# DeltaNet preparation: inverses of two heads in one instruction, half of the decays' rows on ScalarE, transposes one part later, a new order of the parts

## The chip, the cores and the metric

The kernel runs on one core of a Trainium2 chip, in one launch. The metric is the time of the device in microseconds. Five compute engines work from queues of their own and wait for one another by semaphores: TensorE (PE in the profile, with its weight loads as PEld), VectorE (DVE), ScalarE (ACT), GpSimd (POOL) and SyncE (SP), which issues the transfers here. Within one engine, instructions run in the order in which they stand in its queue.

## The reference

One layer of an encoder on 1024 + 256 tokens (two sequences with the same parameters), model width 1024. The mixing half of the layer has two groups: a gated DeltaNet with 4 heads of 128, run forwards and backwards in time, and an attention with 4 query heads and 2 key heads. An output projection and an MLP follow. The change lies in what the DeltaNet needs before its scan:

```python
h = RMSNorm_pre(x); p = h @ w_in
qkv = silu(conv(p_qkv))                 # centred, 5 taps, per channel
q = l2norm(q) * DK ** -0.5;  k = l2norm(k)
diff  = g_cumsum[:, None] - g_cumsum[None, :]
decay = where(lower, exp(diff), 0)      # per chunk, head and direction
kk    = (beta * k) @ k.T * decay
tri   = I + where(strict, kk, 0)
u, w  = solve(tri, [beta * v, beta * k * exp(g)])   # unit lower triangular
a_qk  = (q @ k.T) * decay
# scan over the chunks:  v_new = u - w S;  o = q_d S + a_qk v_new;  S = ...
```

The kernel solves with an explicit inverse of `tri`, in tiles of 128 tokens: 10 tiles, 4 heads, 2 directions.

## The kernel before

The stages of the span are the norm of x with the projection for z and the gates (0 to 111 us), the **preparation** (111 to 536), attention and DeltaNet scan side by side (536 to 800), then the output projection and the MLP. Only the preparation is touched.

It consists of parts, each a generator that is written out step by step. The string `ORDER` (L39 to L43) lists the steps: each entry runs its part up to the next `yield`. Instructions of neighbouring steps lie interleaved in the engines' queues, so a row of the order counts, not the string alone. The parts, for a head h or a column block j:

- **K** (`gdn_qk`): twice a projection with convolution (`conv_proj`), for k and for q. `proj_T` (L350 to L370) casts the weights (`whi` on ScalarE, `wlo` on VectorE at L80), runs 3 x 8 matmuls for each of the token ranges 512, 512 and 256 (`pt`, L367 to L369), and copies to `cp`. After that VectorE adds three taps (L443), GpSimd one (L444), and the SiLU ends on VectorE (L446). TensorE transposes the result by tiles (`kt` L459, `qt` L473), ScalarE takes squares (`gj`, L376) and scaled copies (`kn`, L464) that are stored in `vis_d`.
- **V** (`gdn_v`): the same for v, with transposes `vt` (L502) and copies `vn` (L505).
- **E** (`gdn_e`): five steps of two tiles. `pe` collects a mask (L516) and the decays, whose right-hand sides `ER` (L518) are the mask `incl` times gates: direction 0 on GpSimd, direction 1 on VectorE, 512 columns each. ScalarE takes `E = exp(pe)` (L523). `pk` (L528) is k against k and q; VectorE makes `A` (L529, stored to `vis_d`, one buffer) and `C` (L531).
- **S** (`gdn_sub`): the inverse of all 32 x 32 diagonal blocks of one head. ScalarE copies them (`Cc`, L545), VectorE transposes half (`Ct`, L547), a round trip through `c_d` (L549 to L554) brings them to 80 partitions, one block each. After that there are 31 elimination steps, each a product (`prod`, L560) and an addition (`Rm`, L561) on VectorE and a clearing on GpSimd (L562).
- **L** (`gdn_lev`): a second round trip (`r_d` L569, `Rc` L573, `Rt` L576), and two levels that assemble 64 and then 128 from the blocks (`ph`, `py`, `px`, then `ph2`, `py2`: L589 to L625). The finished `C` is stored at L629 and L630.
- **a** (`att_proj`): a projection for attention. j = 0 to 3 are queries, 4 and 5 keys, 6 and 7 values. The second step transposes (`at`, L400), and for j < 6 turns by the rotary tables (L415 to L417) and, for keys, multiplies by `prk` (L423, L426). The result is stored to `arot_d`; the attention loads it as `ax`.

PSUM has eight banks: three for `pt`, two (`tr`) for `pe` and `pk`, and one each for the transposes of K and V (`tq`), for L (`iv`) and for the attention's transposes (`at`).

Of the kernel before, what the change touches and what calls it, by code (L numbers as in the profile page):

```python
# [20 lines left out]
NT = 10  # L21
# [15 lines left out]


ORDER = (  # L39
    "K0 K0 K0 K0 E0 E0 E0 E0 K1 E0 K1 S0 K1 K1 L0 E1 E1 V0 V0 E1 E1 L0 E1 K2 K2 K2 K2 E2 E2 E2 V1 E2 E2 "  # L40
    "V1 S1 K3 S2 K3 K3 L1 L1 V2 K3 L2 V2 V3 V3 E3 L2 a0 a0 E3 E3 a4 E3 E3 a4 S3 L3 a5 L3 a5 a6 a6 a1 a1 "
    "a2 a2 a3 a3 a7 a7"
)  # L43
# [18 lines left out]
def build(ctx, tc, I, O):  # L62
# [11 lines left out]
    def f32(ap):  # L74
        return ap.bitcast(F32)
# [418 lines left out]
    def gdn_v(h):  # L494
        vT = gp.tile([128, 1282], F32, tag="vT", name="vT", bufs=1)
        yield from conv_proj(8 + h, vT)
        irk = irks[h]
        for t0 in range(0, NT, 4):
            n = min(4, NT - t0)
            tp = tq_tile("vt")  # L500
            for j in range(n):
                T.transpose(tp[:, j * 128:(j + 1) * 128], vT[:, col(t0 + j)], ident)  # L502
            vn = gp.tile([128, 4, 128], F32, tag="kn", name="vn", bufs=3)
            for j in range(n):
                S.activation(vn[:, j], tp[:, j * 128:(j + 1) * 128], AF.Copy, scale=irk[:, t0 + j:t0 + j + 1])  # L505
            SP.dma_start(out=vis_d[h][:, t0:t0 + n, 5], in_=vn[:, :n])

    def gdn_e(h):
# [3 lines left out]
        for t0, n in ((0, 2), (2, 2), (4, 2), (6, 2), (8, 2)):  # L512
            E = gp.tile([128, 2, 2, 128], F32, tag="E", name="E", bufs=2)
            pe = tr_tile("pe").rearrange("p (d j c) -> p d j c", d=2, j=2)
            for d in range(2):
                T.matmul(pe[:, d], lhsT=identr, rhs=nmask[:, 1 - d:2 - d].to_broadcast([128, 2, 128]), start=True, stop=False)  # L516
                R = gp.tile([128, 2, 2, 128], F32R, tag="ER", name="ER", bufs=1)
                (G if d == 0 else V).tensor_tensor(  # L518
                    R, incl[:, d][:, None, None, :].to_broadcast([128, 2, 2, 128]),
                    f32(gr[:, :, t0:t0 + 2, 4 * d + h])[:, :, :, None].to_broadcast([128, 2, 2, 128]), ALU.mult)  # L520
                for i in range(2):
                    T.matmul(pe[:, d], lhsT=(r_gt, r_lt)[d], rhs=R[:, i], start=False, stop=(i == 1))
            S.activation(E, pe, AF.Exp)  # L523
            A = gp.tile([128, 2, 2, 128], F32, tag="A", name="A", bufs=1)
            for j in range(n):
                t = t0 + j
                pk = tr_tile("pk")
                T.matmul(pk[:, 0:256], lhsT=qk[:, 1, col(t)], rhs=qk[:, :, col(t)], start=True, stop=True)  # L528
# [9 lines left out]

    def gdn_sub(h):
        C = Cs[h]  # L540

        Cc = gp.tile([128, 2, NT, 32], F32, tag="Cc", name="Cc", bufs=1)
        for b in range(4):
            bs = slice(32 * b, 32 * b + 32)
            S.mul(Cc[bs], C[bs, :, :, bs].rearrange("p t d c -> p d t c"), -1.0)  # L545
        Ct = gp.tile([128, NT, 32], F32, tag="Ct", name="Ct", bufs=1)
        V.transpose(Ct.rearrange("p t c -> p (t c)"), Cc[:, 0].rearrange("p t c -> p (t c)"))  # L547
        c_d = dr.tile([128, 2, NT, 32], F32, tag="c_d", name="c_d", bufs=2)
        SP.dma_start(out=c_d[:, 0], in_=Ct)  # L549
        SP.dma_start(out=c_d[:, 1], in_=Cc[:, 1])  # L550

        Rm = gp.tile([80, 32, 32], F32, tag="Rm", name="Rm", bufs=2)
        for b in range(4):
            SP.dma_start(out=Rm[20 * b:20 * b + 20], in_=c_d[32 * b:32 * b + 32].rearrange("j d t i -> (d t) j i"))  # L554
        G.memset(Rm.rearrange("p a b -> p (a b)")[:, 0:1024:33], 1.0)
        for p in range(31, 0, -1):
            n = 32 - p
            prod = gp.tile([80, 256], F32, tag="prod", name="prod", bufs=2)
            pv = prod[:, :p * n].rearrange("q (j c) -> q j c", j=p)
            V.tensor_tensor(pv, Rm[:, p, 0:p][:, :, None].to_broadcast([80, p, n]), Rm[:, p:p + 1, p:].to_broadcast([80, p, n]), ALU.mult)  # L560
            V.tensor_tensor(Rm[:, 0:p, p:], Rm[:, 0:p, p:], pv, ALU.add)  # L561
# [933 lines left out]
```

## Time and profile before

| what | value |
|---|---|
| median of 3 runs | 1736.56 us (1734.45 to 1737.36) |
| the profiled execution's own time | 1741.06 us |
| its span, first to last instruction | 1739.3 us |
| mean granted TensorE clock | 0.981 |
| preparation, 111 to 536 us: PE, DVE, ACT, POOL busy | 380.5, 314.5, 226.3, 99.7 us |
| its granted clock and DMA share | 0.96, 0.45 |
| attention and scan, 536 to 800 us: PE busy | 246.1 us |
| from 800 us on: PE busy | 904.6 of 939 us |

"Busy" is the time in which an engine has at least one instruction running. TensorE's instructions overlap, so that their durations add up to more than the time between their starts. A row of a timeline gives start, length, engine, line, operation and tiles, a count where equal instructions follow each other, and in brackets how long the engine stood idle before it and what ended that.

### The profile page before, as it was taken

What the parts mean: (1) busy time and instruction counts of PE and PEld (TensorE: products, weight loads), DVE (VectorE), ACT (ScalarE), POOL (GpSimd) and SP (SyncE); (2) the same over time, 40 slices, a digit from 0 to 9 for tenths busy, and PEclk for the clock granted to TensorE, in tenths of its full rate; (3) what the DMA queues carried; (4) which work ended last, traced back from release to release, by engine and by line L of the source; (5) the groups of instructions that cost most, each with busy time, mean ns of one, the idle gap of its engine ahead of it and who ended that gap; (6) DMA issues with size and microseconds to landing.
All of it is one profiled execution on the core that took longest, in us unless ns stands there. A gap on an engine that the chain in (4) does not pass through costs nothing. (4 is left out here: it accounts for less than half of the span.)

```text
span 1739.3 us, 27944 instructions
## 1 busy us (share of the span) xinstructions
PE 1626.4 (94%) x9799; PEld 1387.8 (80%) x9799; DVE 1267.9 (73%) x2549; ACT 854.6 (49%) x1937; POOL 735.8 (42%) x658
## 2 busy tenths in 40 slices
PE   6999898898997999889988999999989999999997
PEld 5777776777775888668878999999888888888885
DVE  7546798996744778885759954545787978888777
ACT  5236566554345767674446644544465333333422
POOL 3212231321113334440102555554636777788763
PEclk9999999999998999999999999999999999999999
DMA  6113334445447866244333543444556544444234
GB/s 208 70 42 109 97 108 129 137 133 154 133 143 231 273 203 194 79 161 166 104 127 127 178 147 125 151 135 134 187 193 220 154 140 146 132 143 142 86 115 155
DMA packets 208779, 252.68 MB, mean 145 GB/s; under 512 B 35073, under 2 KB 163391, under 8 KB 208639
## 3 DMA queue, kind: packets, MB, share of 16 engines
q1 hardware_dynamic: 208495, 250.77, 45.9%
q8 instruction: 77, 1.26, 0.3%
q14 instruction: 63, 0.52, 0.1%
q0 software_dynamic: 144, 0.13, 0.0%
HBM read 159.75 MB, written 91.10 MB: 144 GB/s over the span
## 5 line engine op out<-in xcount | busy, mean ns | idle before, releaser
L1146 PE MATMUL pd<-mh,ulo 128*128 128x320 f32 x892 | 279.6, 314 | 12.9 <-DVE ulo L80 12.8
L1145 PE MATMUL pd<-mh,uhi 128*128 128x320 f32 x892 | 276.6, 311 | 5.5 <-ACT uhi L79 5.5
L1147 PE MATMUL pd<-ml,uhi 128*128 128x320 f32 x892 | 276.9, 311 | 0.0
L1289 DVE TENSOR_TENSOR acc<-acc,pd 128x512 f32<-128x512 f32 x330 | 206.7, 678 | 44.1 <-PE pd L1285 44.1
L1283 PE MATMUL pd<-dhi,fhi 128*128 128x512 f32 x490 | 192.2, 392 | 1.0 <-DVE acc L1291 1.0
L1284 PE MATMUL pd<-dl,fhi 128*128 128x512 f32 x490 | 192.3, 393 | 0.0
L1285 PE MATMUL pd<-dhi,flo 128*128 128x512 f32 x490 | 191.9, 392 | 0.0
L1146 PEld LDWEIGHTS pd<-mh,ulo 128*128 128x128 f32 x892 | 169.1, 190 | 17.8 <-DVE ulo L80 17.8
L367 PE MATMUL pt<-h_hi,whi 128*128 128x512 f32 (+1 forms) x480 | 178.5, 372 | 0.0
L369 PE MATMUL pt<-h_hi,wlo 128*128 128x512 f32 (+1 forms) x480 | 178.4, 372 | 0.0
L368 PE MATMUL pt<-h_lo,whi 128*128 128x512 f32 (+1 forms) x480 | 178.4, 372 | 0.0
L1145 PEld LDWEIGHTS pd<-mh,uhi 128*128 128x128 f32 x892 | 168.9, 190 | 7.0 <-ACT uhi L79 7.0
L1147 PEld LDWEIGHTS pd<-ml,uhi 128*128 128x128 f32 x892 | 169.0, 190 | 0.0
L1265 ACT CAST fhi<-fr 128x1280 fp32r<-128x1280 f32 x49 | 62.1, 1267 | 212.6 <-PE pd L1284 116.2
L80 POOL TENSOR_TENSOR dl<-dw,dhi 128x1024 fp32r<-128x1024 f32 x49 | 129.0, 2633 | 43.4 <-ACT dhi L79 42.8
L1190 POOL TENSOR_TENSOR s<-u,u 128x320 f32<-128x320 f32 x32 | 34.3, 1071 | 207.6 <-ACT u L1155 140.7
L727 POOL TENSOR_TENSOR P<-P,sm 128x512 f32<-128x512 f32 (+1 forms) x72 | 73.5, 1040 | 95.3 <-DVE sm L725 39.0
L1283 PEld LDWEIGHTS pd<-dhi,fhi 128*128 128x128 f32 x490 | 92.0, 188 | 22.4 <-DVE acc L1291 1.4
L1285 PEld LDWEIGHTS pd<-dhi,flo 128*128 128x128 f32 x490 | 92.0, 188 | 20.7
L1284 PEld LDWEIGHTS pd<-dl,fhi 128*128 128x128 f32 x490 | 92.0, 188 | 20.3
L80 DVE TENSOR_TENSOR ulo<-us,uhi 128x512 fp32r<-128x512 f32 x88 | 76.3, 869 | 43.4 <-ACT uhi L79 42.5
L367 PEld LDWEIGHTS pt<-h_hi,whi 128*128 128x128 f32 x480 | 92.7, 193 | 13.5
(358 smaller groups left out, 4091.0 us busy)
## 6 DMA issues: line engine op xcount, KB each, us to landing
fr<-r_d SPq DMA_DIRECT2D x49, 640.0 KB, 4.3
vis<-vis_d SPq DMA_DIRECT2D x64, 384.0 KB, 4.2
uraw<-in_w_up SPq DMA_DIRECT2D x22, 1024.0 KB, 5.4
r_d<-s SPq DMA_DIRECT2D x128, 160.0 KB, 1.8
r_d<-u SPq DMA_DIRECT2D x96, 160.0 KB, 2.1
dw<-in_w_down SPq DMA_DIRECT2D x28, 512.0 KB, 4.9
wraw<-in_w_in SPq DMA_DIRECT2D x48, 256.0 KB, 3.7
x<-in_x_prompt SPq DMA_DIRECT2D x16, 512.0 KB, 3.4
```

Source lines behind the costliest of these rows:

```text
L80: (V if leng is None else leng).tensor_tensor(lo, src, f32(hi), ALU.subtract)
L367: T.matmul(pm[:, :n], lhsT=whi, rhs=h_hi[:, k, t0:t0 + n], start=(k == 0), stop=False)
L368: T.matmul(pm[:, :n], lhsT=whi, rhs=h_lo[:, k, t0:t0 + n], start=False, stop=False)
L369: T.matmul(pm[:, :n], lhsT=wlo, rhs=h_hi[:, k, t0:t0 + n], start=False, stop=(k == KD - 1))
L727: G.tensor_tensor(x[:, :kw], x[:, :kw], sm[:, 0:1].to_broadcast([128, kw]), ALU.mult)
L1145: T.matmul(pm, lhsT=w[0][:, k], rhs=mh[b, i][:, k], start=(k == 0), stop=False)
L1146: T.matmul(pm, lhsT=w[1][:, k], rhs=mh[b, i][:, k], start=False, stop=False)
L1147: T.matmul(pm, lhsT=w[0][:, k], rhs=ml[b, i][:, k], start=False, stop=(k == 3))
L1283: T.matmul(pm, lhsT=r[0][:, k, tk], rhs=w[0][:, k], start=(k == 0), stop=False)
L1284: T.matmul(pm, lhsT=r[0][:, k, tk], rhs=w[1][:, k], start=False, stop=False)
L1285: T.matmul(pm, lhsT=r[1][:, k, tk], rhs=w[0][:, k], start=False, stop=(k == Q - 1))
L1289: V.tensor_tensor(half(t, d), half(t, d), pm, ALU.add)
```

## The change

Inverses (`gdn_sub`): a part now takes a pair of heads. `Rm` and `prod` get an axis of two, the 62 VectorE instructions become twice as long, and eight steps replace one; `Rm` has one buffer for the pair, `prod` one instead of two.

```diff
+        Rm = gp.tile([80, 2, 32, 32], F32, tag="Rm", name="Rm", bufs=1)
+        for i in range(2):
+            h = 2 * pair + i
...
+                SP.dma_start(out=Rm[20 * b:20 * b + 20, i], in_=c_d[32 * b:32 * b + 32].rearrange("j d t i -> (d t) j i"))
+            Rms[h] = Rm[:, i]
+        G.memset(Rm.rearrange("p h a b -> p h (a b)")[:, :, 0:1024:33], 1.0)
+        yield
         for p in range(31, 0, -1):
             n = 32 - p
-            prod = gp.tile([80, 256], F32, tag="prod", name="prod", bufs=2)
...
-            V.tensor_tensor(Rm[:, 0:p, p:], Rm[:, 0:p, p:], pv, ALU.add)
-            G.memset(Rm[:, p, 0:p], 0.0)
...
+            prod = gp.tile([80, 2, 256], F32, tag="prod", name="prod", bufs=1)
+            pv = prod[:, :, :p * n].rearrange("q h (j c) -> q h j c", j=p)
+            V.tensor_tensor(pv, Rm[:, :, p, 0:p][:, :, :, None].to_broadcast([80, 2, p, n]),
+                            Rm[:, :, p:p + 1, p:].to_broadcast([80, 2, p, n]), ALU.mult)
+            V.tensor_tensor(Rm[:, :, 0:p, p:], Rm[:, :, 0:p, p:], pv, ALU.add)
+            G.memset(Rm[:, :, p, 0:p], 0.0)
+            if p % 5 == 0:
+                yield
```

Decays (`gdn_e`): `ER` has two buffers, direction 0 is made by four ScalarE activations of 128 x 128, and `pk` moves from the ring `tr` to the ring of the transposes.

```diff
-                R = gp.tile([128, 2, 2, 128], F32R, tag="ER", name="ER", bufs=1)
-                (G if d == 0 else V).tensor_tensor(
...
+                R = gp.tile([128, 2, 2, 128], F32R, tag="ER", name="ER", bufs=2)
+                gd = f32(gr[:, :, t0:t0 + 2, 4 * d + h])
+                if d == 0:
+                    for i in range(2):
+                        for j in range(2):
+                            S.activation(R[:, i, j], incl[:, d], AF.Copy, scale=gd[:, i, j:j + 1])
...
-                pk = tr_tile("pk")
+                pk = tq_tile("pk")
```

PSUM: the three single banks become one ring of three.

```diff
-    tq_tile = b_tile("tq", 1)
-    iv_tile = b_tile("iv", 1)
-    at_tile = b_tile("at", 1)
+    tq_tile = iv_tile = at_tile = b_tile("fx", 3)
```

Transposes: K writes the projection for q before it finishes the convolution of k, and has a step more between each convolution and its transposes; V has one more as well.

```diff
-        yield from conv_proj(4 + h, qk[:, 1])
+        pk_, pq_ = conv_proj(4 + h, qk[:, 1]), conv_proj(h, qk[:, 0])
+        next(pk_)
+        yield
+        next(pq_)
+        next(pk_, None)
+        yield
...
-        yield from conv_proj(h, qk[:, 0])
+        next(pq_, None)
+        yield
...
         yield from conv_proj(8 + h, vT)
+        yield
```

Order: the projections for the attention's values (a6, a7) move to the front, without the rotary table, E of heads 2 and 3 stand near each other, and the queries' projections stand among the steps of the second inverse.

```diff
-    "K0 K0 K0 K0 E0 E0 E0 E0 K1 E0 K1 S0 K1 K1 L0 E1 E1 V0 V0 E1 E1 L0 E1 K2 K2 K2 K2 E2 E2 E2 V1 E2 E2 "
-    "V1 S1 K3 S2 K3 K3 L1 L1 V2 K3 L2 V2 V3 V3 E3 L2 a0 a0 E3 E3 a4 E3 E3 a4 S3 L3 a5 L3 a5 a6 a6 a1 a1 "
-    "a2 a2 a3 a3 a7 a7"
+    "K0 K0 K0 V0 K0 K0 V0 E0 K1 E0 V0 E0 E0 K1 E0 K1 a6 K1 K1 a6 E1 a7 E1 E1 a7 E1 E1 V1 S0 K2 S0 V1 S0 K2 S0 V1 S0 K2 "
+    "S0 K2 S0 K2 S0 K3 L0 L0 K3 L1 L1 E2 V2 E2 K3 E2 K3 E2 V2 K3 E2 V2 V3 E3 E3 V3 E3 a4 E3 V3 E3 a4 S1 a5 S1 a5 S1 a0 "
+    "S1 S1 a0 S1 a1 S1 S1 a1 L2 L2 a2 L3 L3 a2 a3 a3"
```

What this makes of the queues is seen at three places. On TensorE, in the last level of head 3 before the change (`px` and `ph_...`, `py_...` are level products, `pt` is a projection):

```order
L369 MATMUL pt<-h_hi,wlo 128x256
L618 MATMUL ph_5086<-X_1017,C 64x64 x10
L369 MATMUL pt<-h_hi,wlo 128x256
L367 MATMUL pt<-h_hi,whi 128x256
L368 MATMUL pt<-h_lo,whi 128x256
L369 MATMUL pt<-h_hi,wlo 128x256
L367 MATMUL pt<-h_hi,whi 128x256
L618 MATMUL ph_5098<-X_1017,C 64x64 x10
```

and after it, where the levels of head 2 end and those of head 3 begin (lines are 16 higher):

```order
L617 MATMUL px<-Hs,Rt 32x32
L634 MATMUL ph_5162<-X_1017,C 64x64
L634 MATMUL ph_5174<-X_1017,C 64x64
L634 MATMUL ph_5162<-X_1017,C 64x64 x9
L634 MATMUL ph_5174<-X_1017,C 64x64 x9
L641 MATMUL py_5186<-C,H_5161 64x64 x10
L641 MATMUL py_5199<-C,H_5161 64x64 x10
L605 MATMUL ph<-Rt,C 32x32 x2
L605 MATMUL ph<-Rc,C 32x32 x2
```

Before, matmuls of a projection stand between the products of a level. Now none does in these two heads, and all projections stand ahead of them.

On ScalarE, in the decays of head 2 before the change (`E` is the exponential, `gj` and `kn` belong to K3, `cy`, `qk` and `cp` to its convolution):

```order
L464 ACTIVATE kn<-kt,cum 128x128 x4
L440 ACTIVATE cy<-cp,cw 128x1282
L523 ACTIVATE E<-pe 128x512
L376 ACTIVATE gj,ssq<-kt 128x128
L441 ACTIVATE qk<-cp,cw 128x1282
```

and after it, at the same decays (K3's transposes for k and q lie here now):

```order
L534 ACTIVATE E<-pe 128x512
L375 ACTIVATE gj,ssq<-kt 128x128
L468 ACTIVATE kn<-kt,cum 128x128 x2
L528 ACTIVATE ER<-incl,gr 128x128
L468 ACTIVATE kn<-kt,cum 128x128 x2
L534 ACTIVATE E<-pe 128x512
L528 ACTIVATE ER<-incl,gr 128x128 x3
L375 ACTIVATE gj,ssq<-qt 128x128
L528 ACTIVATE ER<-incl,gr 128x128
```

The `ER` of the next parts have come in between the scaled copies and squares of the transposes. The kinds ahead of the last `pk` in the whole stretch of head 2's third part to head 3's last are 20 `ER`, 20 `kn`, 20 `gj`, 10 `vn` and 8 `E`.

On SP, the transfers of the second inverse and of its levels after the change, in two pieces; first the loads into `Rm`:

```order
L567 DMA Rm<-c_d 20x32x32 x3
L429 DMA arot_d<-araw 128x1280
L567 DMA Rm<-c_d 20x32x32
L564 DMA c_d<-Ct 128x320
L565 DMA c_d<-Cc 128x320
L393 DMA axw<-aqkv_d 32x1280
L567 DMA Rm<-c_d 20x32x32 x4
```

then the loads into `Rc` for head 3:

```order
L589 DMA Rc<-r_d 32x20x32 x3
L645 DMA vis_d<-C 1280x1x128
L646 DMA vis_d<-C 1280x1x128
L589 DMA Rc<-r_d 32x20x32
L679 DMA ax<-arot_d 128x256
```

A store of `araw` for the keys stands ahead of head 3's `c_d`, and the stores of head 2's finished `C` ahead of the last load of `Rc`. Before the change, an `araw` store stood ahead of `c_d` as well, and all four loads of `Rc` followed each other.

In all, VectorE has 124 instructions fewer, ScalarE 80 more, GpSimd 84 fewer, and TensorE and SP as many as before.

More of the change, by code (lines that the diff above doesn't have):

```diff
@@ L380, in att_proj @@
     def att_proj(j):
-        if not att:
+        if not att and j < 6:
             rope = gp.tile([128, 2, 1282], F32, tag="qk", name="rope", bufs=2)[:, :, 0:1024]
@@ L385, in att_proj @@
             att[0] = rope
-        rope = att[0]
+        rope = att.get(0)
         c = (2064 + j * 128, 2576 + (j - 4) * 128, 2832 + (j - 6) * 128)[max(0, j - 2) // 2]
@@ L516, in gdn_e @@
                 T.matmul(pe[:, d], lhsT=identr, rhs=nmask[:, 1 - d:2 - d].to_broadcast([128, 2, 128]), start=True, stop=False)
-                R = gp.tile([128, 2, 2, 128], F32R, tag="ER", name="ER", bufs=1)
-                (G if d == 0 else V).tensor_tensor(
-                    R, incl[:, d][:, None, None, :].to_broadcast([128, 2, 2, 128]),
-                    f32(gr[:, :, t0:t0 + 2, 4 * d + h])[:, :, :, None].to_broadcast([128, 2, 2, 128]), ALU.mult)
+                R = gp.tile([128, 2, 2, 128], F32R, tag="ER", name="ER", bufs=2)
[4 more added lines that the diff above has]
+                            S.activation(R[:, i, j], incl[:, d], AF.Copy, scale=gd[:, i, j:j + 1])
+                else:
+                    V.tensor_tensor(R, incl[:, d][:, None, None, :].to_broadcast([128, 2, 2, 128]),
+                                    gd[:, :, :, None].to_broadcast([128, 2, 2, 128]), ALU.mult)
                 for i in range(2):
@@ L537, in gdn_e, with gdn_sub @@
         Cs[h] = C
[L539 to L555, printed above, removed]
+    def gdn_sub(pair):
+        Rm = gp.tile([80, 2, 32, 32], F32, tag="Rm", name="Rm", bufs=1)
+        for i in range(2):
+            h = 2 * pair + i
+            C = Cs[h]
+            Cc = gp.tile([128, 2, NT, 32], F32, tag="Cc", name="Cc", bufs=1)
+            for b in range(4):
+                bs = slice(32 * b, 32 * b + 32)
+                S.mul(Cc[bs], C[bs, :, :, bs].rearrange("p t d c -> p d t c"), -1.0)
+            Ct = gp.tile([128, NT, 32], F32, tag="Ct", name="Ct", bufs=1)
+            V.transpose(Ct.rearrange("p t c -> p (t c)"), Cc[:, 0].rearrange("p t c -> p (t c)"))
+            c_d = dr.tile([128, 2, NT, 32], F32, tag="c_d", name="c_d", bufs=2)
+            SP.dma_start(out=c_d[:, 0], in_=Ct)
+            SP.dma_start(out=c_d[:, 1], in_=Cc[:, 1])
+            for b in range(4):
+                SP.dma_start(out=Rm[20 * b:20 * b + 20, i], in_=c_d[32 * b:32 * b + 32].rearrange("j d t i -> (d t) j i"))
+            Rms[h] = Rm[:, i]
+        G.memset(Rm.rearrange("p h a b -> p h (a b)")[:, :, 0:1024:33], 1.0)
+        yield
@@ L556, in gdn_sub @@
         for p in range(31, 0, -1):
             n = 32 - p
-            prod = gp.tile([80, 256], F32, tag="prod", name="prod", bufs=2)
-            pv = prod[:, :p * n].rearrange("q (j c) -> q j c", j=p)
-            V.tensor_tensor(pv, Rm[:, p, 0:p][:, :, None].to_broadcast([80, p, n]), Rm[:, p:p + 1, p:].to_broadcast([80, p, n]), ALU.mult)
-            V.tensor_tensor(Rm[:, 0:p, p:], Rm[:, 0:p, p:], pv, ALU.add)
-            G.memset(Rm[:, p, 0:p], 0.0)
-        Rms[h] = Rm
-        yield
+            prod = gp.tile([80, 2, 256], F32, tag="prod", name="prod", bufs=1)
```

## The prediction

> **What bounds the kernel now.** I read the page's head first, then the busy time by stretch, then what TensorE waits for, then single rows in order of time.
>
> ```profile
> span 1739.3 us, 27944 instructions
> PE 1626.4 (94%) x9799; PEld 1387.8 (80%) x9799; DVE 1267.9 (73%) x2549; ACT 854.6 (49%) x1937; POOL 735.8 (42%) x658
> ...
> 111.00:430.00 319.00, 287.65 (x2217) 231.71 (x2216) 256.32 (x548) 186.36 (x507) 82.30 (x161) 0.97 0.43 118
> 430.00:478.00 48.00, 44.37 (x234) 35.96 (x235) 33.78 (x105) 16.84 (x58) 8.04 (x32) 0.96 0.51 152
> 478.00:512.00 34.00, 32.18 (x407) 26.04 (x406) 16.64 (x40) 14.25 (x44) 5.26 (x3) 0.90 0.35 100
> 512.00:536.00 24.00, 16.32 (x87) 12.87 (x86) 7.74 (x22) 8.85 (x30) 4.12 (x3) 0.87 0.73 221
> ```
>
> The second line is busy time over the span: TensorE (PE) is the bound, VectorE (DVE) comes next. The other rows cut the preparation, the stage that the change touches, into four stretches: length, busy time and count of PE, weight loads, VectorE, ScalarE (ACT) and GpSimd (POOL), granted clock, DMA share, GB/s. What the change can gain is what PE loses in these 425 us, so I counted that.
>
> ```profile
> 424.50 0.70 PE L528 MATMUL pk<-qk 128*128 128x256 f32 x2
> ...
> 157.75 0.40 PE L367 MATMUL pt<-h_hi,whi 128*128 128x512 f32 x1
> 157.98 0.40 PE L368 MATMUL pt<-h_lo,whi 128*128 128x512 f32 x1
> 160.49 0.36 PE L516 MATMUL pe<-nmask,identr 128*128 128x256 f32 x1 [2.11 <-DVE C L531]
> ...
> PE pe L516 <- DVE C L531: 7.6, 6, 2.5
> PE vt L502 <- DVE vT L446: 7.2, 3, 2.6
> PE ps_s L712 <- ACT q_hi L79: 6.1, 1, 6.1
> PE prk L423 <- DVE araw L426: 4.5, 2, 3.1
> PE qt L473 <- DVE qk L446: 3.6, 2, 2.2
> PE pk L528 <- DVE prod L560: 2.3, 1, 2.3
> PE kt L459 <- DVE qk L446: 1.8, 1, 1.8
> PE pe L522 <- DVE ER L518: 1.4, 1, 1.4
> ```
>
> The first row holds the last two `pk` of the preparation, the second of them at about 424.8 us, 313.8 after 111. Dense matmuls of 512 columns start 0.23 us apart (157.75, 157.98), those of 256 half as far. Charging every matmul in those 313.8 us with its dense distance gives an estimated 261 us of work: **about 53 us are lost before the last `pk`**. The list of waits (who, for whom: total, times, longest) names the large ones: transposes that wait for a convolution's last step (`vt`, `qt`, `kt`: 7.2 + 3.6 + 1.8 = 12.6 us), and decays that wait for VectorE (`pe`, `pk`: 7.6 + 2.3 + 1.4 = 11.3 us).
>
> Such waits cost the clock too. Three short stretches, around the wait that ends at 160.49 and behind a later one:
>
> ```profile
> 157.70:161.10 3.40, 1.29 (x8) 0.84 (x8) 3.12 (x17) 1.20 (x1) 0.00 (x1) 1.00 0.00 0
> 161.20:164.60 3.40, 3.40 (x12) 2.90 (x12) 1.66 (x2) 0.59 (x1) 0.00 (x0) 0.50 0.37 117
> 188.50:191.90 3.40, 3.28 (x11) 2.91 (x12) 1.39 (x4) 2.71 (x7) 0.75 (x1) 0.51 0.72 214
> ```
>
> The granted clock is 1.00 while PE waits and 0.50 for the 3.4 us after it, with PE busy throughout: 1.7 us a time. The long stretch has a mean of 0.97, so some 10 of its 319 us go this way; they are within the 53.
>
> The Trainium skill, page "TensorE: Matmul & The Clock Gate", section "HAM oscillation — how this bites in real kernels", says that idle gaps of more than about 3.4 us bring the clock down. The trace differs: a wait of 2.11 us is followed by 0.50. By that rule the change would win no clock here; what it would make of the time is the last rival.
>
> **The change part by part.** *Inverses in pairs.* One head's inverse is 31 steps of two VectorE instructions, each of which needs the one before.
>
> ```profile
> L560 DVE TENSOR_TENSOR prod<-Rm 80x31 f32<-80x31 f32 x8 | 1.5, 184 | 2.5 <-POOL Rm L555 2.4
> L560 DVE TENSOR_TENSOR prod<-Rm 80x256 f32<-80x256 f32 x4 | 1.7, 417 | 0.1
> L518 POOL TENSOR_TENSOR ER<-incl,gr 128x512 fp32r<-128x512 f32 x20 | 29.2, 1462 | 71.0 <-PE pe L522 71.0
> ...
> 254.72 3.20 DVE L80 TENSOR_TENSOR wlo<-wraw,whi 128x512 fp32r<-128x512 f32 x1 [0.22 <-ACT whi L79]
> 254.38 2.99 POOL L444 TENSOR_TENSOR cy<-cy,qk 128x1282 f32<-128x1282 f32 x1 [3.20 <-DVE cy L443]
> 430.01 0.68 DVE L80 TENSOR_TENSOR wlo<-wraw,whi 128x512 fp32r<-128x512 f32 x1
> 135.64 1.03 ACT L464 ACTIVATE kn<-kt,cum 128x128 f32<-128x128 f32 x3
> ```
>
> The first two rows are groups of one shape (count, busy us, mean ns). 31 elements take 184 ns and 256 take 417: about 152 ns for the instruction and 1.04 ns an element. The steps hold 5456 elements (the sum of p x (32 - p)), each in two instructions: 62 x 0.152 + 10,912 x 0.00104 = 9.4 + 11.3 = 20.7 us a head. A pair takes 9.4 + 22.7 = 32.1 instead of 41.4. Ahead of the last `pk` the relief is larger: three heads stand there before (62 us), one pair after (32). VectorE's load there falls from 256 by 30, to 226 us. No PE work hangs directly on this; what it buys is that VectorE reaches the steps that PE waits for earlier.
>
> *Half of `ER` on ScalarE.* Twenty GpSimd operations of 1.46 us go and eighty ScalarE ones come, which the trace does not show. Bounds: nothing (ScalarE is busy only 186 of 319 us) up to 80 x 0.34 = 27 us, by `kn`, three of which take 1.03 us and have the same size. I take 27 us of work, hidden where ScalarE has slack. A GpSimd operation holds up VectorE too: the `wlo` of 254.72 takes 3.20 us, where that of 430.01 takes 0.68, until the GpSimd addition of 254.38 ends. How much of 29 us of `ER` did so is bounded by 0 and 29; I count it into the relief below, not again.
>
> *Transposes one part later, other PSUM ring, `ER` doubled.* No instruction is added. If the later place covers the convolution, 12.6 us of waits go, and the clock windows with them and with the `pe` waits: 10 us at most. The ring of three shared by transposes and `pk` can as well add a wait: bounds are -12.6 and +1.4 (the one short `ER` wait that the doubling can remove, should the ring put it back). I take the whole 12.6, since in the new order a projection stands between.
>
> *The order.* By counting rows ahead of the last `pk`, 1075 matmuls of 512 columns and 560 of 256 stand there now, 992 and 524 before; 83 x 0.233 + 36 x 0.117 = 23.5 us more, less some 4.7 us of small level matmuls that are now later. So the work ahead of the last `pk` is 261 + 18.8 = 280 us. Loss ahead of it: 53 - 12.6 - 11.3 - 10 = 19, less 7 for VectorE's smaller load (a quarter of its 30, an estimate between 0 and 19), plus a new stall of 10. That stall is the burst of `E2` and `E3`: ten decay parts within some 30 us of PE work, where ScalarE has 20 `ER`, 20 `kn`, 20 `gj`, 10 `vn` and 8 `E`, by my estimate 35 to 43 us. Bounds are 5 and 17. Loss after: **22 us**.
>
> Behind the last `pk` stands a chain that PE must wait for. Before, for head 3 (the first two rows are the levels of head 2, from first to last matmul):
>
> ```profile
> 412.02 0.22 PE L589 MATMUL ph<-Rt,C 32*32 32x32 f32 x2
> 423.77 0.80 PE L625 MATMUL py<-C,H 64*64 64x64 f32 x20
> ...
> 428.89 0.60 DVE L531 SCALAR_TENSOR_TENSOR C<-pk,sca,E 128x128 f32<-128x128 f32 x2
> 444.47 0.19 DVE L560 TENSOR_TENSOR prod<-Rm 80x31 f32<-80x31 f32 x1 [2.42 <-POOL Rm L555]
> 478.11 0.19 DVE L561 TENSOR_TENSOR Rm<-Rm,prod 80x31 f32<-80x31 f32 x1
> 492.94 0.84 DVE L576 STREAM_TRANSPOSE Rt<-Rc 128x640 f32<-128x640 f32 x1
> 493.84 0.22 PE L589 MATMUL ph<-Rt,C 32*32 32x32 f32 x2
> 510.18 0.80 PE L625 MATMUL py<-C,H 64*64 64x64 f32 x20
> 535.64 0.80 PE L712 MATMUL ps_s<-k_hi,q_hi 128*128 128x512 f32 x1 [6.13 <-ACT q_hi L79]
> ```
>
> From 424.8 to the first score it takes 110.8 us: 4.7 to the last `C` (429.5), 15.0 to the first `prod`, 33.8 for the inverse with other work between, 15.5 to the levels, 17.2 for them, 24.6 of last projection and attention loads. After: 4 to the last `C`; 18 to the pair's first `prod` (15.0 for one head, 21.5 if the second's loads queue fully); 50 for the pair (32.1, 2 of spacing, 14 of other VectorE rows between, 2 of a GpSimd block); 12 to head 2's levels (15.5 before, where other VectorE work lay between; not under 5, since two transfers follow each other there); 12.5 for those (412.02 to 424.57); 5 until head 3's load has passed head 2's store on SP, which the order puts ahead of it; 12.5 for head 3. That is 114, plus 2 us of transposes that slip into attention: **116 us**, with only some 56 of PE work beside it. The 6.1 us before the first score goes, since the scores' inputs are there by then.
>
> Sum: 111 + 280 + 22 + 116 = 529, against 535.6: **7 us less**, if nothing past it changes (its work is the same). The profiled execution took 1741.06 us, 1.8 more than its span; the runs shown have a median of 1736.56, 4.5 us lower. 1741 - 7 = 1734 profiled, and on the runs' footing **1730 us**.
>
> **The rivals.** *The inverse chain is hidden whole* (0.20). VectorE's relief dissolves the small stalls too, loss 10 rather than 22, and the tail takes 110 as before: 111 + 280 + 10 + 110 = 511, 25 less, 1712. For it: VectorE is 80% busy ahead of the last `pk` before, 71% after. Against: 116 us of chain on 56 of PE work.
>
> *The burst becomes the bound* (0.20, the slower side). `E2` and `E3` run back to back, and `A` has one buffer, which each part must first store:
>
> ```profile
> 171.53 0.42 DVE L529 TENSOR_TENSOR A<-E,pk 128x256 f32<-128x256 f32 x1 [1.62 <-DMA vis_d<-A]
> 177.60 0.41 DVE L529 TENSOR_TENSOR A<-E,pk 128x256 f32<-128x256 f32 x1
> ```
>
> Two parts in a row start 6.1 us apart. Ten of them at 5.5 make 55 us over 30 of PE work: 25 of stall instead of 10, and 7 where the relief does not come: loss 44, 1752. It decides from a cycle of about 4.5 us on. For: the wait for `vis_d<-A` is in the rows. Against: it is there once, 1.6 us.
>
> *The last chain is longer* (0.12). If the pair needs 60 and its loads 22, the tail is 130: 7 us slower than before, 1744. For: an `arot_d` store that waits for a product of `prk` now stands ahead of head 3's `c_d` on SP. Against: head 3's loads took 15.0 with a queue as well.
>
> *The clock windows stay* (0.06). If they come from something other than these short waits, 10 us are not won: 1740. This is where the skill's rule would leave the time; the row at 161.2 is why it has little.
>
> **How the numbers follow.** The forecast has 0.42, with a range of its own of 1720 to 1744 (loss 12 to 36). A measurement here tells about 0.2%, 3.5 us. Faster by more: 0.30 of the forecast and the hidden chain's 0.20, 0.50. Within: 0.09, with 0.02 of the last chain and 0.01 of the clock: 0.12. Slower: 0.03, 0.20, 0.10 and 0.05: 0.38. The range takes in both outer cases, 1709 to 1754.
>
> **What would show it.** VectorE's inverse groups: 62 instructions a pair, near 32 us (right), or above 40 (wrong). The waits of `vt`, `qt`, `kt` under 3 us together. The last `pk` at about 413. Between it and the first score about 116 us, with long waits of `ph` on `Rt`; if these total under 20 us, the chain was hidden. `pe` and `pk` waiting for ScalarE in the burst: 10 us, or 25 if the slower case holds. What would make it wrong most: a loss in the attention or the scan, which I took as unchanged.

## The result, and the profile after

The changed kernel takes 1764.9 us (median of 4 runs, 1761.65 to 1767.37), the kernel before 1736.96 in the same comparison: a ratio of 1.0157, with an interval of 1.0140 to 1.0175. It is slower by 28 us, where 7 us less was forecast, and 11 us above the upper end of the forecast's range, 1754 us. The profiled span went from 1739.3 to 1765.6 us.

To see where, I cut both traces at the same work: at the last `pk` (424.8 before, 422.5 after), at the end of head 3's levels (511.0 and 543.6), and at the matmul that is number 6,200 from the end, in the first scores of the attention (573.6 and 598.1). From there to the end the two run alike: 24.5 us apart at that matmul, 26.4 at the last. First the stretches of before (length, then busy time and count of PE, weight loads, VectorE, ScalarE, GpSimd, then granted clock, DMA share, GB/s):

```profile
111.00:424.80 313.80, 283.75 (x2195) 228.62 (x2195) 251.28 (x540) 184.00 (x502) 79.86 (x161) 0.97 0.43 117
424.80:511.00 86.20, 79.45 (x657) 64.21 (x656) 55.46 (x150) 32.52 (x104) 14.74 (x36) 0.94 0.45 132
511.00:535.60 24.60, 16.96 (x90) 13.38 (x90) 7.74 (x22) 9.79 (x32) 4.78 (x2) 0.88 0.73 224
535.60:573.60 38.00, 34.97 (x205) 28.19 (x206) 23.67 (x56) 23.30 (x71) 15.26 (x14) 0.94 0.82 269
```

and those of after:

```profile
span 1765.6 us, 27828 instructions
PE 1633.7 (93%) x9799; PEld 1401.9 (79%) x9799; DVE 1244.3 (70%) x2425; ACT 875.8 (50%) x2017; POOL 697.8 (40%) x574
...
111.00:422.50 311.50, 295.25 (x2032) 244.68 (x2032) 201.94 (x375) 198.24 (x542) 39.82 (x75) 0.96 0.41 113
422.50:511.50 89.00, 65.06 (x335) 55.66 (x333) 67.42 (x153) 26.60 (x103) 16.18 (x36) 0.87 0.45 133
511.50:543.60 32.10, 17.71 (x569) 14.97 (x570) 14.94 (x31) 15.69 (x36) 2.55 (x2) 0.67 0.46 130
543.60:598.10 54.50, 42.18 (x218) 32.57 (x218) 38.26 (x96) 34.77 (x119) 24.99 (x20) 0.84 0.66 208
```

TensorE's idle time is length less busy time. Ahead of the last `pk` it fell from 30.0 to 16.3 us: there the new order is the better one. Behind it, up to matmul 6,200, it rose from 17.4 (6.8 + 7.6 + 3.0) to 50.6 (23.9 + 14.4 + 12.3). The granted clock is hardly changed in front and lower in every stretch behind.

What TensorE waits for from 111 to 600 us after the change (for whom: total, times, longest):

```profile
PE ph L605 <- DVE Rt L592: 19.6, 2, 10.2
PE prk L422 <- DVE rsa L99: 9.9, 2, 6.0
PE ptr L751 <- POOL P L743: 7.5, 4, 2.0
PE qt L478 <- DVE qk L445: 5.5, 1, 5.5
PE pe L522 <- ACT E L534: 4.2, 2, 2.5
PE at L399 <- ACT araw L369: 3.9, 1, 3.9
...
PE vt L508 <- DVE ngt L98: 1.4, 1, 1.4
```

The waits of transposes for convolutions, 12.6 us before, are 5.5 us of one `qt`; a `vt` waits 1.4 us more for another row of VectorE. New are the levels' waits for `Rt`, 19.6 us. Those of `prk` (4.5 before) and of the attention's transposes `ptr` have grown.

The chain at the end, row by row, on VectorE and TensorE:

```profile
425.52 0.61 DVE L542 SCALAR_TENSOR_TENSOR C<-pk,sca,E 128x128 f32<-128x128 f32 x2
448.63 0.22 DVE L575 TENSOR_TENSOR prod<-Rm 80x62 f32<-80x62 f32 x1 [3.60 <-DMA axw<-aqkv_d]
503.38 0.22 DVE L577 TENSOR_TENSOR Rm<-Rm,prod 80x62 f32<-80x62 f32 x1
512.16 0.27 PE L605 MATMUL ph<-Rt,C 32*32 32x32 f32 x2 [10.24 <-DVE Rt L592]
521.40 1.89 PE L641 MATMUL py<-C,H 64*64 64x64 f32 x39
532.67 0.26 PE L605 MATMUL ph<-Rt,C 32*32 32x32 f32 x2 [9.39 <-DVE Rt L592]
542.17 1.38 PE L641 MATMUL py<-C,H 64*64 64x64 f32 x40 [1.27 <-ACT H L636]
543.48 0.66 PE L399 MATMUL at<-ident,araw 128*128 128x128 f32 x4
549.44 0.76 PE L399 MATMUL at<-ident,araw 128*128 128x128 f32 x4 [2.40 <-ACT gj L375]
555.70 0.63 PE L399 MATMUL at<-ident,araw 128*128 128x128 f32 x2
```

From the last `C` to the first product 22.5 us, the pair's inverse 55.0, then the levels of two heads one after the other with two waits of about 10 us, and only then, from 543.48 to 556, the last transposes of the queries. On SP the chain is held up:

```profile
426.66 1.76 SPq L567 DMA_DIRECT2D Rm<-c_d  x3
438.68 0.35 SPq L429 DMA_DIRECT2D arot_d<-araw  x1
439.07 0.36 SPq L567 DMA_DIRECT2D Rm<-c_d  x1
439.48 0.83 SPq L564 DMA_DIRECT2D c_d<-Ct  x1
```

The fourth `Rm` load of head 2 and `c_d` of head 3, whose data were there at 433, stand behind a store that waits for VectorE's product with `prk`. The loads of `Rc` for head 3 are held up as well (SP's rows, and one of the rows of what SP waits for from 505 to 530 us):

```profile
509.12 0.42 SPq L585 DMA_DIRECT2D r_d<-Rm  x1
518.17 1.43 SPq L589 DMA_DIRECT2D Rc<-r_d  x3
525.13 0.80 SPq L646 DMA_DIRECT2D vis_d<-C  x1
525.97 1.88 SPq L589 DMA_DIRECT2D Rc<-r_d  x1
...
SPq L589 <- PE px L617: 4.2, 1, 4.2
```

`Rc` and `Rt` have one buffer each, before the change and after it. Head 3's first three loads wait until head 2's product `px` has read `Rc`, and the fourth stands behind the stores of head 2's `C`. The second wait for `Rt`, 9.4 us, thus comes from heads 2 and 3 taking turns at one buffer; before the change their levels were some 70 us apart. No run gives these tiles a second buffer.

### The profile page after: what moved, and what is told of

Read it like the earlier page. It is cut to its first block, busy times and chain, and to the rows that moved or that the text cites. A ratio compares the mean times of both kernels' runs of the same rounds, so it can differ in the third digit from the quotient of the medians.

```text
span 1765.6 us, 27828 instructions
## 1 busy us (share of the span) xinstructions
PE 1633.7 (93%) x9799; PEld 1401.9 (79%) x9799; DVE 1244.3 (70%) x2425; ACT 875.8 (50%) x2017; POOL 697.8 (40%) x574
## 5 line engine op out<-in xcount | busy, mean ns | idle before, releaser
L367 PE MATMUL pt<-h_lo,whi 128*128 128x512 f32 (+1 forms) x480 | 175.6, 366 | 0.0
L368 PEld LDWEIGHTS pt<-h_hi,wlo 128*128 128x128 f32 x480 | 91.8, 191 | 15.0 <-DVE wlo L81 0.9
```

The source lines that it names most:

```text
L367: T.matmul(pm[:, :n], lhsT=whi, rhs=h_lo[:, k, t0:t0 + n], start=False, stop=False)
L368: T.matmul(pm[:, :n], lhsT=wlo, rhs=h_hi[:, k, t0:t0 + n], start=False, stop=(k == KD - 1))
```

## The experiments

All are timed in three rounds beside the kernel before, and the ratio is to that. A warning applies to all of them: an edit also changes the order in which the instructions stand, so that a pair of kernels differs in more than the edit. Where that decided something, it is said.

**Single parts undone, or the tail filled.** `e1_single` gives each head of a pair its own instructions:

```diff
+            for i in range(2):
+                prod = gp.tile([80, 256], F32, tag="prod", name="prod", bufs=2)
...
+                V.tensor_tensor(Rm[:, i, 0:p, p:], Rm[:, i, 0:p, p:], pv, ALU.add)
```

> The changed kernel with one thing undone: in each of the 31 steps the two heads of a pair get a product, an addition and a clearing of their own again (124 VectorE instructions a pair, as before the change), at the same places. Theory 1 (the second pair's inverse with the levels of heads 2 and 3 is a chain that TensorE waits for, with too few projections beside it): the second pair takes 9.4 us longer plus some 2 of spacing, all of it on the path, so 8 to 12 us slower than the changed kernel's 1765 (1773 to 1777). Theory 2 (the new pieces, not the order, cost the time: ER on ScalarE, the shared PSUM ring): within 3 us of 1765.

Measured: 1762.92 us, ratio 1.0139 (1.0104 to 1.0174), the same as the changed kernel. The order shifted too: in the profile the second pair's 124 instructions took 48.4 us from first to last, less than the 55.0 of the paired ones, since less other work of VectorE stood between. The waits for `Rt` fell to 6.1 us, and a `qt` in front waited 17.4 instead of 5.5. Theory 1 missed its number, but its condition, a longer inverse, did not come about, so that the run doesn't say what pairing is worth by itself.

`e2_fill` moves two projections into the tail:

```diff
-K1 a6 K1 K1 a6 E1 a7 E1 E1 a7 E1 E1 ... S1 S1 a1 L2 L2 a2 L3 L3 a2 a3 a3
+K1 K1 K1 E1 E1 E1 E1 E1 ... S1 S1 a1 a6 a6 L2 a7 L2 a7 L3 a2 L3 a2 a3 a3
```

> The changed kernel with another place for the two value projections of the attention (a6 and a7): away from the front of the order, ahead of and between the levels of heads 2 and 3. That puts 28 us of projections where TensorE waits. Theory 1: the two waits of ph for Rt (19.6 us) fall under 6 us, the half-clock stretches behind the last pk shrink, and the time falls by 15 to 28 us, to 1737 to 1750. Theory 2: the waits stay elsewhere, time within 5 us of 1765; the front, which loses its filling, gets waits of vt and kt back.

Measured: 1774.22 us, 1.0209 (1.0167 to 1.0251), slower. What TensorE waited for in this kernel:

```profile
PE p L824 <- DMA vis<-vis_d: 17.4, 2, 14.5
PE prk L420 <- DVE rsa L97: 9.9, 2, 6.0
PE ph L603 <- DVE Rt L590: 9.1, 1, 9.1
```

The waits for `Rt` behind the last `pk` went; the one left lies in front, where the projections are missing now. Head 3's levels end at 536 instead of 543.6, but the scan then waits 14.5 us for its loads.

`e3_pool` puts half of `ER` back on GpSimd:

```diff
+                (G if d == 0 else V).tensor_tensor(R, incl[:, d][:, None, None, :].to_broadcast([128, 2, 2, 128]),
```

> The changed kernel with direction 0 of ER back on GpSimd (one operation of 128x512 in place of four ScalarE activations), two buffers kept. Theory 1: within 5 us of 1765, since the tail is not touched. Theory 2 (ScalarE's 80 activations delay the decays of heads 2 and 3): 8 us or more faster, 1757 or less, and the half-clock stretches at 399 and 406 us go.

Measured: 1778.6 us, 1.0229 (1.0193 to 1.0265): 14 us slower than the changed kernel. In this order the ScalarE version of `ER` is a gain, against theory 2.

**The order against the pieces.** `e4_oldorder` has the old order, the old inverse and the other new pieces.

```diff
-    "K0 K0 K0 V0 K0 K0 V0 E0 ... a1 L2 L2 a2 L3 L3 a2 a3 a3"
+    "K0 K0 K0 K0 K0 E0 E0 E0 E0 K1 E0 K1 K1 S0 K1 K1 L0 ... S3 L3 a5 L3 a5 a6 a6 a1 a1 a2 a2 a3 a3 a7 a7"
```

> The old order of the parts and the old inverse (one head a part), with the other new pieces: ER on ScalarE with two buffers, the shared ring of three with pk in it, the query projection written ahead of the key convolution. Theory 1 (the order costs the time): 1730 to 1743, no slower than before the change. Theory 2 (the pieces cost it): 1755 or more.

Measured: 1821.25 us, 1.046 (1.0411 to 1.0508). One row of its waits says why:

```profile
PE ph L598 <- DVE Rt L585: 54.7, 3, 26.6
```

This led to theory 3, on the PSUM ring. `e5_banks` and `e6_iv1` (new order), `e7_old_banks` and `e8_old_iv1` (old order) take the ring apart:

```diff
-    tq_tile = iv_tile = at_tile = b_tile("fx", 3)
+    tq_tile = b_tile("tq", 1)
+    iv_tile = b_tile("iv", 1)
+    at_tile = b_tile("at", 1)
...
-                pk = tq_tile("pk")
+                pk = tr_tile("pk")
```

That is the edit of `e5_banks` and `e7_old_banks`; `e6_iv1` and `e8_old_iv1` take out the levels alone:

```diff
-    tq_tile = iv_tile = at_tile = b_tile("fx", 3)
+    tq_tile = at_tile = b_tile("fx", 2)
+    iv_tile = b_tile("iv", 1)
```

> The changed kernel with PSUM as before the change: one bank each for the transposes of K and V (tq), for the levels (iv) and for the attention's transposes (at), and pk in the ring of two with pe. Theory 3 (the shared ring of three makes each transpose and each pk wait behind a level's tile that was taken earlier, so that TensorE stands still while the levels wait for Rt): in the new TensorE order all transposes of the queries stand ahead of the levels of heads 2 and 3, what is lost behind them goes, and the time falls by 12 us or more, to 1753 or less. Theory 1 (the chain of the second inverse on too few projections): the waits of ph for Rt stay near 20 us and the time within 6 us of 1765.

Measured: 1766.83 us, 1.0179 (1.0149 to 1.0209), no change against the changed kernel. The waits for `Rt` fell to 8.6 us, though, and others took their place (11.1 us for `whi`, 6.6 of `kt`).

> The changed kernel with a bank of its own for the levels only; transposes and pk share a ring of two. Theory 3: like e5_banks, 1753 or less. Theory 1: within 6 us of 1765.

Measured: 1785.82 us, 1.0285 (1.0254 to 1.0317), 21 us slower than the changed kernel, which neither theory had.

> The kernel e4_oldorder (old order, one head an inverse, 1821 us) with PSUM as before the change. What is left of the change is ER on ScalarE with two buffers and the query projection written ahead of the key's convolution. Theory 3: the waits of ph for Rt (54.7 us) fall under 8 us and the time to 1732 to 1745. Theory 2 (ER on ScalarE, or the split of K and V): 1765 or more.

Measured: 1749.43 us, 1.0071 (1.0044 to 1.0099).

> The kernel e4_oldorder with a bank of its own for the levels only, transposes and pk in a ring of two. Theory 3: 1732 to 1748, as e7_old_banks. If it stays above 1765 while e7_old_banks falls, it is pk among the transposes that costs, not the levels.

Measured: 1752.9 us, 1.0096 (1.0066 to 1.0125).

In the old order the shared ring costs some 70 us: taking the levels out of it brings 1821 to 1753, all the way back 1749, and the waits for `Rt` are no longer among the large ones (in e7, 13.2 us of `vt` lead the list). In the queue of `e4_oldorder` the transposes of six of the attention's eight parts stand behind the levels of head 3, and no projection stands among those levels; in that of `e7_old_banks` projections stand among them, and the transposes of only two parts behind their beginning. My reading is that a tile of the ring that was handed to a level ties what is handed out next to that level's wait. In the new order the same two edits bring nothing (`e5_banks`) and cost 21 us (`e6_iv1`): giving the levels a bank of their own does not win back what the changed kernel loses. Theory 3 holds for the old order alone.

`e11_er` is the kernel before with `ER` on ScalarE and nothing else of the change; its edit is the one that the change makes in `gdn_e`, without that of `pk`.

> The kernel before the change with one part of it: direction 0 of ER by four ScalarE activations, two buffers of ER. If ER on ScalarE is what e7_old_banks (1749) pays for: 1745 or more. If it gains as in the changed kernel (where undoing it cost 13 us): 1735 or less.

Measured: 1772.91 us, 1.0185 (1.0158 to 1.0211): one part alone costs the old kernel 34 us. Three rows of its waits up to 430 us:

```profile
PE vt L502 <- DVE vT L446: 8.5, 2, 6.6
PE qt L473 <- ACT gj L376: 7.8, 2, 6.1
PE vt L502 <- ACT vn L505: 5.3, 6, 1.2
```

The waits for `gj` and `vn` were 0.4 and 0.2 us in the kernel before. With one bank for these transposes, TensorE waits until ScalarE has read the tile before, and ScalarE now has `ER` to make as well. That is some 13 of the 34 us. The low clock grew too, from 20.5 us ahead of the last `pk` to 61.4; what else the 34 us hold was not taken apart.

`e12_later` and `e15_later_pool` write transposes one entry later in the old order:

```diff
-E1 E1 V0 V0 V0 E1 E1 L0 E1 ... E2 E2 V1 E2 E2 V1 V1 S1 K3 S2
+E1 E1 V0 V0 E1 V0 E1 L0 E1 ... E2 E2 V1 E2 E2 V1 S1 V1 K3 S2
```

> The kernel e7_old_banks (old order, old inverse, old PSUM; 1749 us) with the transposes of V and of two of the K parts written one entry of the order later. If waits of transposes for convolutions are worth what they last, vt's 13.2 us of waits fall under 4 us and the time by 8 to 13 us, to 1736 to 1741. If the waits move elsewhere, the time stays within 4 us of 1749.

Measured: 1745.77 us, 1.0033 (1.0020 to 1.0046). The waits of `vt` fell from 13.2 to 9.7 us, not under 4, and the time by 3.7, with intervals that touch: the second expectation.

> The kernel e12_later (old order, old PSUM, transposes of V and of two K parts one entry later; 1746 us) with ER as before the change, on GpSimd and with one buffer. What is left of the change is the later transposes and the split of K. If ER on ScalarE is what the old order pays for (e11_er: 34 us): 1725 to 1737, faster than before the change. If ER costs nothing here: 1743 to 1749.

Measured: 1745.52 us, 1.0041 (1.0022 to 1.0059), the same as `e12_later`. Here `ER` on ScalarE costs nothing. Much the same edit is thus worth +34, 0 and -14 us, by what stands around it.

**The queues.** `e9_sq` and `e10_sqlev` issue transfers of the inverses, and then of the levels too, from ScalarE:

```diff
-            SP.dma_start(out=c_d[:, 0], in_=Ct)
+            S.dma_start(out=c_d[:, 0], in_=Ct)
```

> The changed kernel with the round trip of the inverses (the stores c_d and the loads of Rm) issued by ScalarE's queue and not by SP's. In the changed kernel head 2's last Rm load and head 3's c_d stand on SP behind a store of araw that waits for VectorE's product with prk, and are issued 6 to 16 us after their data are there. Theory 4 (SP's queue holds up the second inverse): from the last C to the first product of the second pair 22.8 us become 13 to 16, the levels end 7 to 10 us earlier and the time falls by 5 to 10 us, to 1755 to 1760. Theory 1 (the chain on VectorE and TensorE alone): within 3 us of 1765.

Measured: 1766.28 us, 1.0146 (1.0115 to 1.0177). The first product of the second pair came 24 us after the last `C`, no earlier than before. Theory 4 is not borne out, but neither is it settled: ScalarE's queue held the loads up in its turn (the fourth of head 2 was issued at 429.7, those of head 3 from 437 to 441.5), and GpSimd's clearing of the diagonal, which the first product waits for, stood behind a rotation's addition of 451.0 to 453.9.

> As e9_sq, and the round trip of the levels (r_d, Rc) and the stores of the finished C also by ScalarE's queue. Theory 4: SP is free for the attention's loads behind the preparation as well: another 5 to 10 us, 1745 to 1755. Theory 1: the levels of heads 2 and 3 stay where they are, within 4 us of e9_sq; if ScalarE's queue waits for these transfers instead, it is slower than e9_sq.

Measured: 1773.12 us, 1.0187 (1.0159 to 1.0215). That is 7 us above `e9_sq`, with intervals that overlap; another 5 to 10 us less, as theory 4 had it, is excluded.

`e16_fill_st` is `e2_fill` with the stores of `C` issued from ScalarE:

```diff
-        SP.dma_start(out=vis_d[h][:, :, 1], in_=C[:, :, 1])
+        S.dma_start(out=vis_d[h][:, :, 1], in_=C[:, :, 1])
```

> The kernel e2_fill (a6 and a7 in the tail; 1774 us) with the stores of the finished C issued by ScalarE's queue. In e2_fill SP stood 12.3 us at such a store, with the loads for attention and scan behind it, and TensorE then waited 14.5 us for vis. If that is what e2_fill lost again: that wait goes and the time falls by 10 to 18 us, to 1756 to 1764. If not: within 5 us of 1774.

Measured: 1762.03 us, 1.0142 (1.0121 to 1.0163), 12 us less than `e2_fill`, as expected. In place of `vis`, TensorE now waited 10.8 us for the first query (`q_hi`).

**The chain at the end.** `e13_noinv` and `e14_nolev` leave work out (which, their expectations say):

```diff
+            if pair == 1 and p > 4:
+                if p % 5 == 0:
+                    yield
+                continue
```

> The changed kernel with 27 of the 31 elimination steps of the second pair (heads 2 and 3) left out; first pair, loads, levels and all else stay. Theory 1 (the chain at the end is the price): the levels of heads 2 and 3 no longer wait, projections of the queries run between them, and the time falls by 15 to 30 us, to 1735 to 1750. If the price lies elsewhere (in front, or in the shared ring), it stays above 1757.

Measured: 1768.26 us, 1.0177 (1.0158 to 1.0196): nothing gained. The levels did not stop waiting, as theory 1 had it. The inverse was done at 452.9, but head 2's last `Rc` loads left SP only at 485.4, behind a store that waited 8.4 us for a rotation on GpSimd, and its levels began at 492.4. The second wait for `Rt`, between the two heads, stayed: 10.1 us. Head 3's levels ended at 525, 18 us earlier than in the changed kernel, but a projection and transposes of the queries now stood behind them, and the scores waited for those:

```profile
539.25 1.25 PE L399 MATMUL at<-ident,araw 128*128 128x128 f32 x10
547.70 0.80 PE L732 MATMUL ps_s<-k_hi,q_hi 128*128 128x512 f32 x1 [7.20 <-ACT q_hi L80]
```

The levels go in the second of the two kernels:

```diff
+        if h >= 2:
+            yield
+            SP.dma_start(out=vis_d[h][:, :, 1], in_=C[:, :, 1])
+            SP.dma_start(out=vis_d[h][:, :, 8], in_=C[:, :, 0])
+            return
```

> The changed kernel with the levels of heads 2 and 3 left out (their round trip, their products and the writing back into C); C is stored as it is after the decays. The inverse of the pair stays, and nothing waits for it. Theory 1: the two waits for Rt (19.6 us) and the levels at half clock (some 20 us) go, and with them most of the loss: the time falls by 25 to 40 us, to 1725 to 1740. If the price lies elsewhere: it falls by no more than the levels' dense work, 9 us, to 1756 or above.

Measured: 1743.43 us, 1.0029 (1.0018 to 1.0041): 21.5 us less than the changed kernel, a little under the expected 25 to 40. From the last `pk` to matmul 6,200 it took 144.6 us (426.1 to 570.7), against 175.6 for the changed kernel and 148.8 for the kernel before. Here too the scores wait for the queries, and longer:

```profile
PE ps_s L733 <- ACT q_hi L80: 16.6, 1, 16.6
```

`e17_late_lev` and `e18_single` ask why the levels cost more than their matmuls:

```diff
-... S1 S1 a1 L2 L2 a2 L3 L3 a2 a3 a3
+... S1 S1 a1 a2 a2 a3 a3 L2 L2 L3 L3
```

> The changed kernel with the last entries of the order changed alone: a2 a2 a3 a3 stand ahead of L2 L2 L3 L3. On TensorE all transposes of the queries then stand ahead of the levels, and scores between the levels of heads 2 and 3. If the levels cost 22 us because transposes, rotations and loads of the attention wait behind them: the scores start within 6 us of e14_nolev's (529), the levels run beside the softmax, and the time falls by 12 to 22 us, to 1743 to 1753. If the levels' own chain is the price wherever it stands: within 5 us of 1765.

Measured: 1766.04 us, 1.0170 (1.0148 to 1.0191). All transposes stood ahead of the levels and were done at 503.4; then TensorE stood still:

```profile
PE ph L603 <- DVE Rt L590: 21.9, 2, 21.6
```

The first score stood at 534.8, within the expected 6 us of 529. At matmul 6,200 from the end this kernel was 15.5 us behind the kernel before, against 24.5 for the changed one; by the end the difference was 23.9 again, and what it lost there was not looked into.

In the other kernel T2 and T3 are the inverses of one head each:

```diff
-... V3 E3 E3 V3 E3 a4 E3 V3 E3 a4 S1 a5 S1 a5 S1 a0 S1 S1 a0 S1 a1 S1 S1 a1 L2 L2 a2 L3 L3 a2 a3 a3
+... V3 T2 E3 E3 V3 E3 T2 a4 E3 V3 T2 E3 a4 T2 T3 a5 T2 a5 T3 L2 a0 T3 L2 a0 T3 a1 T3 a1 a2 L3 a2 L3 a3 a3
```

> The changed kernel with an inverse of its own for head 2 and for head 3 (62 VectorE instructions each, in four steps); head 2's starts among the decays of head 3, and head 2's levels stand beside head 3's inverse. If the pair makes both heads late and that is the price: head 2's levels end 30 us or more earlier, only one wait for Rt is left at the end, and the time falls by 8 to 18 us, to 1747 to 1757. If it is what stands behind the levels: within 5 us of 1765.

Measured: 1770.34 us, 1.0187 (1.0159 to 1.0215). Head 2's levels ended at 501 instead of 523, and the waits for `Rt` fell to 7.0 us. From the last `pk` to matmul 6,200 this kernel took 162.5 us instead of 175.6, as much less as was expected. But its last `pk` came 10 us later, at 432.6, with the first steps of head 2's inverse now ahead of it, and behind matmul 6,200 it took 7 us longer. So the time did not follow.

No version beat the kernel before; the nearest complete ones are `e12_later` and `e15_later_pool`.

## Why the prediction was wrong, step by step

The sum was 111 + 280 of work + 22 of loss + 116 behind the last `pk` = 529. The same point of the work came at 560 in the trace (535.6 + 24.5). Three terms carry the 31 us between: 10.5, 7.1 and 14.5 us, less 1 us of work.

*Loss ahead of the last `pk`: 22 forecast, some 32.5 by the same count.* The trace holds 83 matmuls of 512 columns and 36 of 256 more than before, less one head's levels, as forecast, so that the work is 279 of the 311.5 us. The `pk` came at 422.5, not 413. The waits behaved as forecast. Without the clock the loss fell from 43 to some 20 us, where the terms had taken 20.9 away (12.6 + 11.3 + 7 less 10). The term that failed is the clock. I took all of the 10 us as won, because each low stretch followed a wait. There are fewer waits now, but the clock of the stretch is 0.96 and not 0.97, 4% of 311.5 or 12 us: nothing was won. The five low stretches in it (at 283.6, 324.6, 365.5, 399.7 and 406.5) each come within 5 us of the start of a wait of 1.4 to 5.5 us, and three of them last 6.8 us and not 3.4. Why fewer waits brought as much low clock stays open.

The rival in which the clock windows stay (0.06) had this term's size right. The rule of the Trainium skill, page "TensorE: Matmul & The Clock Gate", section "HAM oscillation — how this bites in real kernels", which wants no idle gaps above about 3.4 us, would also have left those 10 us where they were, since the waits taken away were shorter. This trace doesn't bear it out: four of the five low stretches follow waits of 1.4 to 2.5 us.

*The chain behind the last `pk`: 114 forecast, 121.1 measured.* Term by term, forecast and measured: 4 and 3.6 to the last `C`; 18 and 22.5 to the first product; 50 and 55.0 for the pair; 12 and 8.6 to head 2's levels; 12.5 and 11.1 for these; 5 and 9.4 until head 3's; 12.5 and 10.9. The mechanisms are those of the text (the `arot_d` store on SP is in the rows above), but for the one buffer of `Rc`, which the 5 us until head 3's levels left out, and the sizes are off by 7. The pair's instructions took 37.5 us in the trace, the 32.1 worked out and two blocks by GpSimd additions (3.2 and 3.1 us where 0.4 to 0.7 was due).

*Behind the chain: 2 forecast, 16.5 measured.* From the first score to matmul 6,200 it was 38.0 before; from the end of head 3's levels to it, it is 54.5. Here the step failed: "the 6.1 us before the first score goes, since the scores' inputs are there by then", and so did the size of the 2 us for transposes that slip into the attention. The first score did stand at 534.2, between the levels. But the order shown ahead of the prediction has the last transposes behind the levels; they, the rotations of two queries and their loads run in the first part of the attention, which has VectorE, ScalarE and GpSimd for its softmax. Of the 16.5 us, 9.3 are idle time of TensorE (12.3 against 3.0), and the low clock takes some 5 more (17.1 us of low stretches against 4.5). The longest waits are those of `ptr` for GpSimd's `P`, 7.5 us in the list above. Before the change they were (535 to 575 us):

```profile
PE ptr L735 <- POOL P L727: 2.0, 4, 0.8
```

One of them after the change, followed back, goes from `ptr` to `P` on GpSimd, to the softmax's sum `sm` on VectorE, and there to a rotation that waits for the last transposes:

```profile
556.36 0.48 DVE L414 SCALAR_TENSOR_TENSOR araw<-araw,nw,rope 128x256 f32<-128x256 f32 x1 [0.77 <-PE at L399]
556.91 0.16 DVE L741 RECIPROCAL sm<-sm 128x1 f32<-128x1 f32 x1
557.22 2.04 POOL L743 TENSOR_TENSOR P<-P,sm 128x512 f32<-128x512 f32 x2 [4.48 <-DVE sm L741]
558.31 0.44 PE L751 MATMUL ptr<-ident,P 128*128 128x128 f32 x2 [1.99 <-POOL P L743]
```

GpSimd has the rotations' additions besides (count, busy us, mean ns, idle before, from 540 to 600 us):

```profile
L416 POOL TENSOR_TENSOR araw<-araw,axw 128x1280 f32<-128x1280 f32 x2 | 5.8, 2893 | 1.6 <-DVE sm L740 1.6
```

The kernel before has none there.

Of the other rivals, none was it. *The burst* did not come: `pe` waits 4.2 us for ScalarE. *The last chain is longer* named the mechanism of 7 us of the 31. *Hidden whole* is refuted by TensorE's idle time from the last `pk` to the end of head 3's levels, 38.3 us. The sign that I gave for it, waits for `Rt` under 20 us, would have said the opposite with its 19.6; the threshold was badly set. The `ER` activations took 0.41 us each, 28.7 us busy in all, close to the 27 taken.

What the runs show of the cause: taking the levels of heads 2 and 3 away from the end takes away 21.5 us of 28 (`e14_nolev`). Leaving out the inverse of that pair takes away nothing (`e13_noinv`), since SP's queue and the one buffer of `Rc` held the levels up in its place. In the new order both heads' levels stand between the last projections and the attention in TensorE's queue. Three things stay open. The levels' own matmuls are in the 21.5 (my estimate was 9 us), so that how much of it is waiting is not measured. A second buffer for `Rc` and `Rt` was not tried. And no order of these parts was found in which the loss goes: filling the tail (`e2_fill`, `e16_fill_st`), the levels behind the transposes (`e17_late_lev`) and two single inverses (`e18_single`) each shortened the wait they aimed at and lost elsewhere: to `vis`, `q_hi`, one `Rt` of 21.6 us, a later `pk`. These runs suggest that the end of the preparation has several chains of nearly equal length, and I had summed one.

## What to carry to other kernels

Before an order is judged by the waits that it removes, list what stands behind the last long chain in each engine's queue, which tiles of it have one buffer, and where the next stage's inputs come from: a gain of some 20 us in front (53 to 32.5 us of loss) was paid back more than twice over there, where the stretch became 26.8 us longer with some 18 us less of work. In a kernel whose queues are ordered by the builder, one edit has no price of its own (+34, 0 and -14 us for much the same one), so that its worth is measured in the order in which it is to stand. A ring of buffers shared by tiles that wait long and tiles that don't can tie their order together: it cost 70 us in one order, and in another taking it apart won nothing.

## What the runs showed of the hardware

In these traces the low clock lasts in multiples of 3.4 us (3.4, 6.8, 10.2 and 17.1 us in the changed kernel, apart from the last stretch of its span, which the end cuts), and small matmuls did not always end it. Two stretches of the changed kernel:

```profile
444.10:450.90 6.80, 5.72 (x24) 5.46 (x25) 2.86 (x12) 0.00 (x0) 0.65 (x4) 0.50 0.84 214
505.50:522.60 17.10, 7.62 (x265) 7.20 (x266) 7.55 (x16) 5.94 (x13) 0.00 (x0) 0.50 0.56 146
```

In the second, 265 matmuls ran in 17.1 us, and the clock was 0.50 throughout. It cost the levels little: head 2's took 11.1 us here, and head 0's, in the same kernel and at full clock, 9.2. So a low clock says little of what is lost where TensorE waits for others in each step.
